# One gate of the gated MLP moved to the next stage, its mixing in another set of banks, one bias operation for two heads

## The chip, the core and the metric

The kernel runs on one core of a Trainium2 chip. The metric is the time of one execution on the device in microseconds; the median of three runs before the change is 690.52 us.

## What is computed

A layer norm of x (1024 x 1024), then one mixer layer: a combined projection of 3912 columns feeds four head groups, each multiplied by its own gate, concatenated, projected out and normalised. Cut to what matters here:

```
proj = x @ w_in + b_in            # a_u a_v a_g | bq bk bv bg | cq ck cv cg | iq ik iw | mq mg
ya = gelu(a_u) * (W_s LN(gelu(a_v)) + b_s)         # A: 128 x 128 mixing per channel group
yb = softmax(q k' / 8 + relative bias) v           # B: own chunk and 8 chunks before, 4 heads
score = sum_h relu(iq_h . ik / 8) * iw_h / sqrt(8) # index scores of 8 heads
idx = top 256 keys of each query by score          # C: attention to those alone, 4 heads
yc = softmax(q k_idx' / 8 + bias[idx]) v_idx
ym = softmax(q km' / 8) vm                         # M: 256 memory tokens, 4 heads
mixed = concat(ya * silu(a_g), yb * silu(bg), yc * silu(cg), ym * silu(mg))
out = LN(alpha * x + mixed @ w_out + b_out)
```

All is float32; a projection is made of three matmuls per 128 rows of weights (high part times high part, high times low, low times high).

## The kernel before, in words

The work lies in stages that follow each other in program order, and the framework draws the order of each engine's queue at compile time: it takes instructions by their place in the program (earlier is more urgent; some blocks are raised or lowered) as soon as they are ready in its own simulated time. The engines then run these fixed queues in order. So an instruction of a later stage can stand as filling between those of an earlier one.

**Index stage** (line 516). The words of `INDEX_ORDER` (line 56) are done in turn: `q2` projects a pair of index queries (`iq_tile`, line 455: one load of weights, projections of 256 and 512 columns), `h1` forms the scores of a pair of index heads for all keys (`index_heads`, line 462: matmuls into two banks per piece, relu on ACT, weighted sum on DVE), `a0` is the first half of group A's gate (`gate_of_a`, line 485): two weight blocks, for each half of the positions a gelu of a_u and a silu of a_g, their product on POOL and its store to DRAM. `a1` is the second half and stands in `EARLY`, with the second pair of memory gates `m0`, `m1`.

**The stage that follows** (line 1105): `early_steps` runs `EARLY` and the projection of the memory queries. It is woven (`weave`, line 657) with the search for the 256th largest score: `search` (line 977) settles one bit of a threshold per step. A step ("test" below) writes `cand`, counts scores above it (three blocks of rows on ACT as `jka`, three on DVE as `jk`) and settles `bit` and `thr`. Search steps have the lowest priority of all (`PRI`), and a step may not stand ahead of what was last on DVE and ACT four parts (`LAG_S`) before it. `PACE` says how many steps go with each of five weaves: the early steps, the memory attention of two pairs of heads, the band attention (B) of two pairs. `count` (line 1110) is the number of parts of the first weave, 8 for each projection.

**The two weaves of memory attention** take as filling the projections for A's v rows and for B (`first_filler`, `second_filler`, lines 919 and 938). Between them stand four groups of A's mixing (`a_mix`, line 823): 16 matmuls into one bank `pm`, an add of the table on DVE (`amix`), a product with the stored gate on POOL, a store.

**Banks.** PSUM's eight banks are shared by name (`BANKS`, line 68): `pp` 2 (projections, and here the mixing), `qk` 2 and `pt` 3 (scores of the first and second head of a pair; `pt` also serves every second product with V, all turning of tiles, and gating), `pv` 1.

**Band and sparse attention** (`mix_of`, line 703). `scores` writes the scores of two heads, adds bias and keeps running maxima in `mx` (one DVE operation per piece and head), then for each head forms the Exp's bias `nb` = 14 ln 2 - max on DVE and calls Exp on ACT. In group B, POOL splits the result in two 16-bit parts, and a DMA turns it.

Of the kernel before, what the change touches and what calls it, by code (L numbers as in the profile page):

```python
# [18 lines left out]
AF = mybir.ActivationFunctionType  # L19
ALU = mybir.AluOpType  # L20
# [4 lines left out]
P = 128  # L25
# [8 lines left out]
PSHIFT = 14.0 * math.log(2.0)  # L34
# [18 lines left out]
HR_S4 = 3  # L53
WO_V = 2
LAG, LAG_T, LAG_S, LAG_C = 22, 15, 4, 6
INDEX_ORDER, EARLY = "h0 q2 h1 a0 q3 h2 h3", "a1 m0 m1"
B0_ORDER, B1_ORDER, C0_PROJ = "g0 v1 g1 k0 k1", "q0 q1 k0 k1 v0 g0 v1 g1", "k0 k1 q0 q1 v0 g0 v1 g1"
RATES = (48, 64, 64, 64)
PRI = 10 ** 6
PACE = ((6,), (8,), (8,), (11,), (16,))  # L60
MASKS = (6, 7, 5), (4, 3, 2)
C1_STEPS = 40
C1_ORDER, C1_HELD, HELD_PARTS, HELD_STEPS = "k0 k1 v1 q1 v0 g1", "q0 g0", 5, 16
# [15 lines left out]
def tile_trunk(ctx, tc, x, mem, ln_in_g, ln_in_b, w_in, b_in, a_ln_g, a_ln_b, a_ws, a_bs,  # L79
# [23 lines left out]
    PE, V, S = Engine(nc.tensor), Engine(nc.vector), Engine(nc.scalar)  # L103
# [33 lines left out]
    bias = cp.tile([P, 31], F32, name="bias")  # L137
# [33 lines left out]
    def small(shape, name, bufs=3):  # L171
        return gp.tile(list(shape), F32, tag=name, bufs=bufs, name=name)
# [13 lines left out]
    def bank(tag, name=None):  # L186
        return ps.tile([P, 512], F32, tag=tag, bufs=BANKS[tag], name=name or tag)
# [82 lines left out]
    def two_banks():  # L270
        return bank("qk"), bank("pt", "qk")

    def pieces_of(n):
        return {640: ((0, 384), (384, 640)), 768: ((0, 384), (384, 768)), 896: ((0, 384), (384, 896)),
                1024: ((0, 512), (512, 1024))}.get(n, ((0, n),))
# [252 lines left out]
    def spread(pt, n):  # L528

        t = gp.tile([P, 10, P], F16, tag="pT", bufs=TB, name="pT")  # L530
        ph, pl = [t[:, a:a + 4].rearrange("p j q -> p (j q)") for a in (0, 4)]
        S.activation(ph[:, :n], pt[:, :n], AF.Copy)
        V.tensor_sub(pl[:, :n], pt[:, :n], ph[:, :n])
        return [ph[:, j * P:(j + 1) * P] for j in range(n // P)], [pl[:, j * P:(j + 1) * P] for j in range(n // P)]
# [168 lines left out]
    def mix_of(kt, rb, kb0, st, near, far_of, last):  # L703

        by_dma = kt < 4
        q, k, v3 = st
        nk = rb + 1 - kb0
        n = nk * P
        nfar = max(0, n - 256)
        chunks = list(range(0, nk, 4))  # L710
        d = {}

        def scores():
            d["rsum"] = small([P, 2], "rsum", 5)
            d["sc"] = [gp.tile([P, 1024], F32, tag="S", bufs=SB, name="sc") for _ in range(2)]
            mx = [small([P, 4], "mx", 4) for _ in range(2)]
            nr = [near(odd) for odd in range(2)]
            nmx = [0, 0]
            pieces = [(a, b) for a, b in pieces_of(n)]
            for group in [pieces] if by_dma else [[piece] for piece in pieces]:  # L720
                banks = [two_banks() if by_dma else (bank("qk"), bank("qk")) for _ in group]
                two_heads(q, k, [(accs, 0, b - a, rb * P, kb0 * P + a) for accs, (a, b) in zip(banks, group)])
                for (a, b), accs, odd in [(*x, odd) for x in zip(group, banks) for odd in range(2)]:
                    for lo, hi in ((a, min(b, nfar)), (max(a, nfar), b)):
                        if lo >= hi:
                            continue
                        other = far_of(lo, hi) if hi <= nfar else nr[odd][:, 256 - n + lo:256 - n + hi]
                        i = nmx[odd]
                        V.tensor_tensor_reduce(d["sc"][odd][:, lo:hi], accs[odd][:, lo - a:hi - a], other, 0.125,
                                               mx[odd][:, i - 1:i] if i else -3e38, ALU.add, ALU.max, mx[odd][:, i:i + 1])  # L730
                        nmx[odd] += 1
            for odd in range(2):
                sc, i = d["sc"][odd], nmx[odd]
                nb = small([P, 1], "nb")
                V.tensor_scalar(nb, mx[odd][:, i - 1:i], -1.0, PSHIFT, ALU.mult, ALU.add)
                S.activation(sc[:, :n], sc[:, :n], AF.Exp, bias=nb, accum_out=d["rsum"][:, odd:odd + 1])
                if by_dma:
                    d["p", odd] = turned(sc, n)

        def turn(odd, c):  # L740
            sc = d["sc"][odd]
            m = min(4, nk - c)
            pt = bank("pt")
            for j in range(m):
                PE.transpose(pt[:, j * P:(j + 1) * P], sc[:, (c + j) * P:(c + j + 1) * P], ident)
            d["p", odd, c] = spread(pt, m * P)

        def values(odd, c):
            if not odd and not c:
                d["pv"] = bank(("pv", "pt")[rb % 2 and by_dma], "pv")  # L750
            ph, pl = [part[c:] for part in d["p", odd]] if by_dma else d["p", odd, c]
            for j in range(min(4, nk - c)):
                pv_mm(d["pv"], odd, ph[j], pl[j], v3[:, kb0 + c + j, odd], c + j == 0, c + j == nk - 1)
            if odd and c == chunks[-1]:
                d["o"] = normalized(d["pv"], d["rsum"], kt)

        def close():
            last(lambda dst: gated(d["o"], gate_of(kt, rb), dst))

        steps = [(odd, c) for odd in range(2) for c in chunks]  # L760
        return [Item(scores, [] if by_dma else [lambda s=s: turn(*s) for s in steps], [lambda s=s: values(*s) for s in steps], close)]


# [59 lines left out]
    def a_mix(vts, i, r2):  # L823
        if i not in gates_a:
            gates_a[i] = [gp.tile([P, 512], F32, tag="near", bufs=2, name="gate_a") for _ in range(2)]
            for p in range(2):
                SP.dma_start(out=gates_a[i][p], in_=gate_dram[p][i])
        pm = bank("pp", "pm")
        for r in range(2):
            for g in range(4):  # L830
                PE.matmul(pm[64 * (g % 2):64 * (g % 2) + 64, (2 * r + g // 2) * P:(2 * r + g // 2 + 1) * P],
                          vts[:, r, g * 64:g * 64 + 64], wsT[:, g, :], start=True, stop=True)
        t = ev("amix").rearrange("p (r t c) -> p r t c", r=2, t=2)
        V.tensor_add(t, pm.rearrange("p (r t c) -> p r t c", r=2, t=2), bsT.unsqueeze(1).to_broadcast([P, 2, 2, P]))
        for r in range(2):
            rb = 4 * i + 2 * r2 + r
            for p in range(2):
                G.tensor_mul(t[:, r, p], t[:, r, p], gates_a[i][p][:, (rb % 4) * P:(rb % 4 + 1) * P])
            SP.dma_start(out=mix_dram[rb][:, 0:2, :], in_=t[:, r])
# [131 lines left out]
    for i, rb in enumerate(RBS):  # L971
        n = (rb + 1) * P
# [84 lines left out]
    for i, rb in enumerate(RBS):  # L1057
        n = (rb + 1) * P
# [43 lines left out]
    def pace(i):  # L1102
        return [(f, n) for f, n in zip(topk, PACE[i])]

# [274 lines left out]
```

## Time and profile before

| | before |
|---|---|
| median of 3 runs | 690.52 us (689.62 to 691.79) |
| profiled execution | 689.95 us, its span 688.2 us |
| mean granted TensorE clock | 0.982 |
| PE busy | 644.5 us, 94% |
| DVE busy | 516.0 us, 75% |
| ACT busy | 392.8 us, 57% |
| POOL busy | 351.6 us, 51% |

Busy times are of one execution under the hardware profiler. A PE row's end is modelled, and rows of matmuls that follow each other overlap. Engines: PE matmuls, PEld weight loads, DVE vector, ACT scalar, POOL GpSimd, SP the queue that issues DMAs. All operations on PE, DVE and ACT go through one recorder and carry its line, L94, so groups are told apart by the names of their tiles: `acc` a projection, `qk` scores, `pm` the mixing, `amix` its add.

### The profile page before, as it was taken

The numbers are of one execution on the slowest core, as the hardware profiler recorded it, in microseconds if no ns is written. First come the engines' busy times: TensorE is split into PE (matmuls) and PEld (weight loads), VectorE is DVE, ScalarE is ACT, GpSimd is POOL, SyncE is SP. The second block draws the span as 40 slices with busy tenths as digits, with TensorE's granted clock in tenths as the row PEclk, the third lists the DMA queues.
The fourth block names the chain that finished last, engine by engine and source line by source line (L and its number), as shares of the span: only waits on it lengthen the run. The fifth ranks groups of instructions, "written<-read, shape, count | busy, mean of one in ns | idle before, by whom it ended". The sixth has DMA issues, their size and how long they took to land.

```text
span 688.2 us, 11110 instructions
## 1 busy us (share of the span) xinstructions
PE 644.5 (94%) x3698; PEld 487.8 (71%) x3698; DVE 516.0 (75%) x1286; ACT 392.8 (57%) x801; POOL 351.6 (51%) x362
## 2 busy tenths in 40 slices
PE   4989999999999985979989999999999999999995
PEld 3857876776777764767767766677777777777785
DVE  6585245655777897899799789996567789889735
ACT  4665336554777867875978886444345474444210
POOL 3672311631538775474556355984222455559752
PEclk9999999999999997999999999999999999999998
DMA  9792610411236442445356535654001564143111
GB/s 275 232 335 68 168 31 1 122 32 47 72 96 123 97 126 62 86 118 142 79 108 144 94 92 107 131 98 117 30 21 54 162 198 171 65 136 148 63 61 62
DMA packets 121669, 75.30 MB, mean 109 GB/s; under 512 B 58976, under 2 KB 111500, under 8 KB 121612
## 3 DMA queue, kind: packets, MB, share of 16 engines
q1 hardware_dynamic: 121612, 74.59, 39.9%
q8 instruction: 29, 0.48, 0.3%
q14 instruction: 28, 0.23, 0.1%
HBM read 46.44 MB, written 17.64 MB: 93 GB/s over the span
## 4 chain that ended last, share of the span: by engine, by line
PE 53%; DVE 20%; ACT 8%; issue 5%; DMA 2%; POOL 2%; DVEq 0%; POOLq 0%; SPq 0%; ACTq 0%
PE acc L94 40%; PE qk L94 7%; ACT jka L94 4%; DVE jk L94 4%; PE pv L94 4%; PE pt L94 2%; DVE sc L94 2%; DVE o L94 2%; DVE nb L94 2%; DVE cand L94 1%; DMA raw<-in_w_in 1%; ACT sc L94 1%; DVE thr L94 1%; DVE bit L94 1%; DVE vt L94 1%
## 5 line engine op out<-in xcount | busy, mean ns | idle before, releaser
L94 PE MATMUL acc<-hTh,wblk 128*128 128x512 f32 (+1 forms) x960 | 324.3, 405 | 12.9 <-DVE amix L94 11.5
L94 PEld LDWEIGHTS acc<-hTh,wblk 128*128 128x128 f32 x960 | 180.3, 192 | 61.8 <-DVE amix L94 12.3
L94 PE MATMUL acc<-hTl,wblk 128*128 128x512 f32 (+1 forms) x480 | 191.3, 399 | 0.0
L206 POOL TENSOR_TENSOR wblk<-raw,wblk 128x512 fp32r<-128x512 f32 x72 | 99.5, 1386 | 95.9 <-ACT wblk L94 93.9
L94 ACT ACTIVATE jka<-score,cand 128x768 int8<-128x768 f32 (+2 forms) x93 | 96.7, 1040 | 21.9 <-DVE cand L94 19.5
L94 PEld LDWEIGHTS acc<-hTl,wblk 128*128 128x128 f32 x480 | 92.3, 192 | 18.7 <-issue 1.4
L94 ACT ACTIVATE sc<-sc,nb 128x640 f32<-128x640 f32 (+7 forms) x64 | 46.6, 731 | 48.0 <-DVE nb L94 34.4
L94 PEld LDWEIGHTS <-pT 128*128 128x128 f16 x656 | 45.4, 98 | 29.5 <-issue 21.5
L94 DVE SCALAR_TENSOR_TENSOR score<-relu,iw,score 128x384 f32<-128x384 f32 (+5 forms) x42 | 44.8, 1071 | 20.7 <-ACT relu L94 18.1
L94 ACT ACTIVATE wblk<-raw 128x512 fp32r<-128x512 f32 x72 | 44.6, 627 | 24.3 <-PE acc L94 17.2
L544 POOL TENSOR_TENSOR sc<-sc 128x512 f16<-128x512 f32 (+4 forms) x48 | 57.1, 1196 | 1.8
L94 PE MATMUL pv<-v,pT 128*128 128x192 bf16 (+1 forms) x528 | 54.6, 234 | 1.5 <-DMA pT<-sc 1.5
L94 PE MATMUL acc<-woh,mh 128*128 128x512 f32 (+1 forms) x144 | 55.6, 386 | 0.0
L94 PE MATMUL acc<-woh,ml 128*128 128x512 f32 (+1 forms) x144 | 53.5, 373 | 0.2 <-DVE nb L94 0.2
L94 PE MATMUL acc<-wol,mh 128*128 128x512 f32 (+1 forms) x144 | 53.6, 372 | 0.0
L94 ACT ACTIVATE relu<-qk 128x384 f32<-128x384 f32 (+2 forms) x80 | 36.2, 527 | 26.5 <-PE qk L94 26.3
L543 POOL TENSOR_SCALAR sc<-sc 128x512 f16<-128x512 f32 (+4 forms) x48 | 33.8, 708 | 33.2 <-ACT sc L94 32.8
L94 ACT ACTIVATE pT<-pt 128x512 f16<-128x512 f32 (+3 forms) x48 | 22.3, 483 | 36.6 <-PE pt L94 33.4
L94 DVE TENSOR_SCALAR_CACHE_REDUCE jk<-planes,lo 128x384 bf16<-128x384 uint16 (+2 forms) x48 | 35.7, 744 | 1.1
L94 PE MATMUL qk<-kh,qh 64*128 64x384 f32 (+3 forms) x96 | 31.9, 411 | 2.6 <-DVE mx L94 1.6
L94 DVE TENSOR_SCALAR_CACHE_REDUCE jk<-planes,cand 128x384 bf16<-128x384 bf16 (+2 forms) x45 | 33.3, 739 | 0.6
L1146 POOL TENSOR_TENSOR comb<-score,nearC 128x256 f32<-128x256 f32 x24 | 18.5, 784 | 27.1 <-DVE mx L94 24.8
(205 smaller groups left out, 1250.3 us busy)
## 6 DMA issues: line engine op xcount, KB each, us to landing
raw<-in_w_in SPq DMA_DIRECT2D x32, 512.0 KB, 3.7
xt<-in_x SPq DMA_DIRECT2D x8, 512.0 KB, 4.6
h_dram<-xt SPq DMA_DIRECT2D x8, 512.0 KB, 5.6
gate<-t SPq DMA_DIRECT2D x16, 256.0 KB, 2.0
rawo<-in_w_out SPq DMA_DIRECT2D x8, 512.0 KB, 4.8
hr<-h_dram SPq DMA_DIRECT2D x8, 512.0 KB, 4.6
out<-hr SPq DMA_DIRECT2D x7, 512.0 KB, 2.6
gate<-gate SPq DMA_DIRECT2D x48, 64.0 KB, 2.0
```

The source lines that it names most:

```text
L94: ins = op(*a, **k)
L206: G.tensor_sub(t[:, 1], r, f32(t[:, 0]))
L543: G.tensor_scalar(high, sc[:, :n], 1.0, 0.0, ALU.mult, ALU.add)
L544: G.tensor_sub(rest, sc[:, :n], high)
L1146: G.tensor_add(t, score[rb][:, n - 256:n], nearC[pair][:, odd, :])
```

## The change

Three edits. The word `a0` goes from the index stage's order to the front of `EARLY`, so that the search's first weave has 96 parts instead of 64; `PACE` is drawn anew, with the same total of 49 steps. The mixing's bank `pm` is taken from `pt` instead of `pp`. In `mix_of`, the maxima of both heads lie in one tile, and one DVE operation forms the biases of both before either Exp; the tile `mx` has three buffers for two heads (before: four for one), `nb` three for two heads (before: three for one).

```diff
-INDEX_ORDER, EARLY = "h0 q2 h1 a0 q3 h2 h3", "a1 m0 m1"
+INDEX_ORDER, EARLY = "h0 q2 h1 q3 h2 h3", "a0 a1 m0 m1"
...
-PACE = ((6,), (8,), (8,), (11,), (16,))
+PACE = ((10,), (7,), (7,), (10,), (15,))
...
-            mx = [small([P, 4], "mx", 4) for _ in range(2)]
+            mx = small([P, 2, 4], "mx")
...
                         V.tensor_tensor_reduce(d["sc"][odd][:, lo:hi], accs[odd][:, lo - a:hi - a], other, 0.125,
-                                               mx[odd][:, i - 1:i] if i else -3e38, ALU.add, ALU.max, mx[odd][:, i:i + 1])
+                                               mx[:, odd, i - 1:i] if i else -3e38, ALU.add, ALU.max, mx[:, odd, i:i + 1])
                         nmx[odd] += 1
+            nb = small([P, 2], "nb")
+            V.tensor_scalar(nb, mx[:, :, nmx[0] - 1], -1.0, PSHIFT, ALU.mult, ALU.add)
             for odd in range(2):
-                sc, i = d["sc"][odd], nmx[odd]
-                nb = small([P, 1], "nb")
-                V.tensor_scalar(nb, mx[odd][:, i - 1:i], -1.0, PSHIFT, ALU.mult, ALU.add)
-                S.activation(sc[:, :n], sc[:, :n], AF.Exp, bias=nb, accum_out=d["rsum"][:, odd:odd + 1])
+                sc = d["sc"][odd]
+                S.activation(sc[:, :n], sc[:, :n], AF.Exp, bias=nb[:, odd:odd + 1], accum_out=d["rsum"][:, odd:odd + 1])
...
-        pm = bank("pp", "pm")
+        pm = bank("pt", "pm")
```

## Rows read from the trace of the kernel before

**Rows 1.** The page, part 1: busy us, share of span, instructions.

```profile
PE 644.5 (94%) x3698; PEld 487.8 (71%) x3698; DVE 516.0 (75%) x1286; ACT 392.8 (57%) x801; POOL 351.6 (51%) x362
```

**Rows 2.** Busy time by stage: stretch, length, each engine, clock, DMA share, GB/s.

```profile
84.00:187.00 103.00, 102.89 (x560) 74.98 (x556) 60.58 (x74) 56.80 (x118) 31.70 (x24) 1.00 0.19 54
187.00:308.00 121.00, 106.54 (x633) 82.47 (x629) 101.50 (x265) 94.34 (x208) 78.46 (x101) 0.96 0.44 102
308.00:331.00 23.00, 23.00 (x105) 17.86 (x106) 20.89 (x58) 14.92 (x28) 11.69 (x16) 0.93 0.48 124
331.00:450.00 119.00, 114.40 (x664) 81.87 (x663) 107.97 (x370) 86.21 (x175) 71.54 (x76) 0.99 0.51 106
450.00:650.00 200.00, 196.88 (x1175) 147.03 (x1174) 161.22 (x400) 92.38 (x199) 104.38 (x90) 0.99 0.35 109
```

**Rows 3.** Chain of waits, shares by line, of 84:187, 187:308 and 308:331.

```profile
by line: PE acc L94 73.0%; PE qk L94 24.1%; ACT t L94 1.2%; issue 0.6%; ACT wblk L94 0.6%; PE wst L94 0.6%; ACT xh L94 0.0%
...
by line: ACT jka L94 15.4%; DVE jk L94 11.1%; issue 8.5%; DVE nb L94 7.6%; DVE vt L94 5.6%; PE acc L94 5.2%; DVE cand L94 4.6%; DVE thr L94 4.3%; ACT sc L94 4.0%; ACT score L94 3.8%; DVE bit L94 3.6%; DVE score L94 3.2%; DMA raw<-in_w_in 2.
...
by line: PE acc L94 89.5%; PE pv L94 5.0%; PE qk L94 2.5%; PE vt L94 1.9%; PE pt L94 1.5%
```

**Rows 4.** PE in order of time: start us, us, what, count.

```profile
93.74 0.39 PE L94 MATMUL acc<-hTl,wblk 128*128 128x512 f32 x1
...
94.44 0.40 PE L94 MATMUL acc<-hTl,wblk 128*128 128x512 f32 x1
...
201.50 0.51 PE L94 MATMUL qk<-km,mqh 64*128 64x256 f32 x4
```

**Rows 5.** Chain of waits, pieces of the index stage: start us, us, what.

```profile
132.29 7.29 PE acc L94 x37
...
156.37 3.70 PE acc L94 x15
```

**Rows 6.** DVE in order of time: starts of tests of the search.

```profile
195.44 0.17 DVE L94 TENSOR_SCALAR cand<-thr 128x6 uint32<-128x6 uint32 x1
...
205.68 0.17 DVE L94 TENSOR_SCALAR cand<-thr 128x6 uint32<-128x6 uint32 x1
...
324.44 0.16 DVE L94 TENSOR_SCALAR cand<-thr 128x6 uint32<-128x6 uint32 x1
...
329.03 0.17 DVE L94 TENSOR_SCALAR cand<-thr 128x6 uint32<-128x6 uint32 x1
```

**Rows 7.** Groups of instructions, DVE: count, busy us, mean ns, idle before.

```profile
L94 DVE TENSOR_SCALAR_CACHE_REDUCE jk<-planes,cand 128x384 bf16<-128x384 bf16 (+2 forms) x45 | 33.3, 739 | 0.6
...
L94 DVE SCALAR_TENSOR_TENSOR t<-t,xh 128x512 f32<-128x512 f32 x24 | 20.4, 852 | 8.9 <-ACT t L94 8.9
...
L94 DVE TENSOR_SCALAR cand<-thr 128x6 uint32<-128x6 uint32 x31 | 11.0, 356 | 0.6
...
L94 DVE TENSOR_TENSOR bit<-c,bar 128x6 uint32<-128x6 f32 x31 | 10.9, 351 | 17.2 <-ACT jka L94 16.9
...
L94 DVE SCALAR_TENSOR_TENSOR thr<-bit,thr 128x6 uint32<-128x6 uint32 x31 | 9.2, 296 | 0.6
...
L94 DVE TENSOR_SCALAR nb<-mx 128x1 f32<-128x1 f32 x64 | 8.1, 144 | 0.0
```

**Rows 8.** Waits: who, for whom, us in all, times, longest.

```profile
PE acc L94 <- DVE amix L94: 11.5, 3, 6.9
```

**Rows 9.** In order of time: the mixing's add, projections that waited for it.

```profile
267.61 0.69 DVE L94 TENSOR_TENSOR amix<-pm,atab 128x512 f32<-128x512 f32 x1
...
268.35 0.80 PE L94 MATMUL acc<-hTh,wblk 128*128 128x512 f32 x1 [6.90 <-DVE amix L94]
...
307.98 0.80 PE L94 MATMUL acc<-hTh,wblk 128*128 128x512 f32 x1 [3.68 <-DVE amix L94]
```

**Rows 10.** DVE in order of time: a bias, then a score operation.

```profile
333.19 0.15 DVE L94 TENSOR_SCALAR nb<-mx 128x1 f32<-128x1 f32 x1
333.26 0.42 DVE L94 CUSTOM_DVE_ANT_0 sc<-qk,nearB 128x256 f32<-128x256 f32 x1
```

## The prediction

> **What bounds the kernel now.** I read the page's two first parts, then a table of busy time by stage, then the chain of waits in each stage, then single stretches. The page has PE at 94% and DVE at 75% [rows 1], which alone would say: PE sets the time, and work that only moves from one stretch of PE to another is worth nothing. The table and the chain say something else. In 84:187, the index stage, PE is busy 102.89 of 103 us and DVE 60.58 [rows 2], and the chain is PE: 73.0% projections, 24.1% index scores [rows 3]. In 187:308, the search with the memory attention, DVE is busy 101.50 of 121 and ACT 94.34, and the chain is spread over the search's tests on ACT (15.4%) and DVE (11.1%) and a tail of small DVE steps; PE's projections have 5.2% of it. In 308:331 the chain is PE again (89.5%). In 331:450 DVE is busy 107.97 of 119. In 450:650 PE is busy 196.88 of 200. So the bound alternates: PE, DVE with ACT, PE, DVE, PE.
>
> PE's busy share also overstates it: two hTl matmuls with two others between them start 0.70 us apart, so one takes 0.233 us of the array, while its own row says 0.39 [rows 4]. The Trainium skill (Perfetto Trace Analysis, Identifying the Most-Contended Engine) says the same, that matmul busy time is no measure of headroom and weight-load time is the better one; the page's 71% for weight loads [rows 1] agrees. By the 94% the move would give nothing (the third rival below), by the 71% PE has room in 187:308.
>
> **The sum's base.** The profiled execution took 689.95 us (span 688.2, 1.75 around it), 0.57 under the median of 690.52. Terms are taken from 689.95; at the end 0.57 is added. A measurement of this kernel tells about 0.3% (2.1 us) from no change.
>
> **Part 1: the gate a0 leaves the index stage.** It is 4 projections of 24 matmuls, 96 x 0.233 = 22.4 us of PE, and two weight blocks, four evictions, two POOL products and two stores with it. It does not vanish: the same matmuls now have lower priority than q3, h2 and h3, as a1, m0 and m1 have today. Those already run inside the index stage as filling: between two bursts of index scores PE does 15 projection matmuls in 3.70 us [rows 5]. Filling is still at hand (a0 takes the place that a1 has), so I expect the heads h1 to h3 to keep their rhythm. What goes is the one place where PE does nothing but projections on the way to the last index score: 37 matmuls, 7.29 us from 132.29, the end of a0 and all of q3, which h2 follows [rows 5]. q3 then becomes filling of h0 and h1. So the last index score comes 7.3 us sooner (bounds: 0, if a0 only changes places with q3; 22.4, if none of a0 is done before the last score).
>
> The first memory scores, at 201.50 [rows 4], do not come sooner: all projections in front of them are the same, and PE stands at none of them. So in these 7.3 us the search works on DVE and ACT beside PE's projections. A test of the search beside projections took 4.6 us (324.44 to 329.03 [rows 6]); 7.3 / 4.6 = 1.6 tests are done early. Today one test starts (195.44) before 201.50 and the second at 205.68, although six are allowed in that weave, so it is the late scores and not PACE that hold the search; I cost the new PACE at nothing for that reason. It costs as much as the lead is worth if the tests do come as fast as it allows. In 187:308 DVE is in the chain, so each test that is gone from it gives back its DVE time: 3 counts x 0.739 + 0.356 + 0.351 + 0.296 = 3.2 us [rows 7]. 1.6 x 3.2 = **-5.1 us** (bounds: 0 to -15.6, that is 22.4 / 4.6 = 4.9 tests).
>
> Moved with it: the evictions are four t products of 0.852 us on DVE [rows 7], now perhaps beside the search. Before 201.50 DVE is idle for 42 of 103 us [rows 2], so I cost them at nothing; without that cover, +3.4. The two weight loads are moved past that of q3 in SP's queue and their splits past q3's on ACT and POOL; both engines are about half idle or more in 84:187 (56.80 and 31.70 of 103), so nothing is added. The two stores of a0 go later in SP's queue; their reader, the product behind the mixing's adds, stands far behind (the second add is at 267.61 [rows 9]).
>
> **Part 2: the mixing's bank.** The four a_mix groups today take one of the two pp banks of the projections and hold it until DVE adds the table. DVE has the search queued in front of that add. PE waits for it three times, 11.5 us in all, the longest 6.9 [rows 8]: at 268.35 it had waited 6.90 for the add of 267.61, at 307.98 another 3.68 [rows 9]. With a bank from the three of pt, the next projection finds a pp bank free. For the first two waits I count nothing: they lie inside the stretch whose chain is DVE and ACT. The third opens the stretch 308:331, which is PE alone; there 3.7 us are **-3.7 us**. The granted clock is 0.93 in that stretch [rows 2], 1.6 us of 23 that may come back as well; I leave it out, since the clock is also under 1 in 331:450 where no mixing is. Bounds: 0 (the wait moves to another bank) to -11.5 - 1.6 = -13.1.
>
> By the Trainium skill (Perfetto Trace Analysis, Matmuls) independent groups should rotate through different banks, so that one's eviction overlaps the next one's matmuls. By it the whole 11.5 would go, and that sum is a rival below.
>
> **Part 3: one bias operation.** 64 nb operations become 32. They take 8.1 us in all, 0.127 each [rows 7]; 16 of those removed lie in 331:450, where DVE is the bound: -2.0. The other 16 lie behind 450, beside PE: nothing. Against it, the first head's Exp now waits until the second head's scores are written. Often both nb stand back to back; where they don't, as behind 333.19, a score operation of 0.42 us lies between [rows 10], and ACT, then POOL's split and the turning DMA of the first head come 0.4 later. If that were so 16 times and always in the chain, +6.7. Taking it for a few places, I put the part at **-1.0 us** (bounds -2.0 and +4.7).
>
> **Sum.** 689.95 - 5.1 - 3.7 - 1.0 = 680.15, and with 0.57 for the median 680.7 us.
>
> **The rivals** (times with the 0.57).
> - *The index stage empties.* PE's order may put none of a0 in front of the last index score. For it: a0 has the lowest priority of what stands there. Against: a1 with the same priority fills today, and a matmul costs nothing where PE would wait for ACT to free a bank. Lead 22.4 us, 4.9 tests, -15.6 - 3.7 - 1.0: 670.2 us.
> - *All mixing waits are worth their length.* If PE, running ahead in 250:308, brings the projections of the band stage forward so that the PE-bound stretch 308:331 begins that much earlier and is that much shorter, all 11.5 us count: 689.95 - 5.1 - 11.5 - 1.0 + 0.57 = 672.9. For it: that stretch is made of exactly these projections. Against: they can run ahead only as far as two pp banks and their evictions on DVE allow, and DVE is the one that is late. It is the result that the rotation rule above would give.
> - *Nothing moves.* PE's work is the same, the lead is eaten since the attention's own steps on ACT, POOL and DMA, not the search, set 187:308, and PE picks up its waits elsewhere; what is left is part 3: 690 (688.5 to 691). For it: 94% PE on the page; tests stand in the chain with small pieces only, the largest share being 15.4%. Against: rows 2 and 3.
> - *Slower: the mixing stops the attention.* pt also serves the second head's scores, every second PV product, every gating transpose and the turning of V and of the gate rows. A pt bank that waits for DVE behind the search can hold up one of these instead of a projection, and behind that PE instruction, in order, stand the scores that DVE, ACT and POOL wait for. Price: the 11.5 us that PE waits today, now in the chain: 689.95 + 11.5 - 5.1 - 1.0 + 0.57 = 695.9. It decides from the point at which PE asks for a third pt bank between a mixing and its add. For it: the add was up to 6.9 us late and each memory item asks for pt four times. Against: three banks, and at 268.35 what PE wanted next was a projection.
>
> **How the numbers follow.** Forecast 680.7 (own range 674 to 687): 0.43. Emptied index stage: 0.10. All mixing waits: 0.10. Nothing moves: 0.17, of which 0.02 go to faster. Slower: 0.20. Faster by over 0.3%: 0.43 + 0.10 + 0.10 + 0.02 = 0.65; within 0.3%: 0.15; slower: 0.20. For 8 in 10 the range must reach most of the faster rivals (670.2) and of the slower one (695.9) with some room for the order of all queues being drawn anew: 668 to 697.
>
> **What would show it.** Part 1: in the profile after, no run of 37 projection matmuls between h1 and h2, the last index score near 180 instead of 187, the first memory scores still near 201, and the third test started by then. If the last index score is near 165, the first rival. Part 2: the row of waits of PE's projections for amix gone, and no wait of some us for a pt bank (by the add, by a gating product or by nb) in its place; the stretch between the end of memory attention and the first band scores begins and ends earlier. Part 3: 32 nb operations of about the same 0.13 us. The prediction is wrong if the first memory scores come later than 202, if PE waits for DVE in 250:310 as long as before, or if the gain that is there at 331 is given back by 450, since the tests that are then still to come lie in the band stage.

## The result, and the profile after

The changed kernel takes 686.24 us (median of 6 runs, 684.75 to 688.17) against 690.60 (6 runs); the ratio is 0.9935, 95% interval 0.9915 to 0.9954. Timed again later beside other runs of before it was 0.9968 (0.9950 to 0.9986). So it is faster, by 0.3 to 0.65%, 2 to 4.5 us; forecast were 9.8. The two timings of this one kernel differ by 0.33%, so in what follows a difference of that size between kernels timed apart is at the edge of what can be told. The profiled execution has a span of 685.0 us, before 688.2. The table by stage, as [rows 2] (the page's first row first):

```profile
PE 641.4 (94%) x3698; PEld 485.2 (71%) x3698; DVE 523.8 (76%) x1254; ACT 390.8 (57%) x801; POOL 349.9 (51%) x362
...
84.00:187.00 103.00, 100.01 (x554) 74.02 (x553) 69.17 (x96) 60.71 (x123) 28.16 (x22) 1.00 0.17 47
187.00:308.00 121.00, 114.34 (x671) 88.50 (x669) 101.78 (x257) 95.64 (x215) 82.94 (x103) 0.99 0.46 106
308.00:331.00 23.00, 22.05 (x117) 16.12 (x116) 22.00 (x71) 15.25 (x31) 11.11 (x16) 1.00 0.59 147
331.00:450.00 119.00, 111.82 (x645) 79.96 (x641) 104.73 (x324) 79.69 (x163) 70.97 (x76) 0.97 0.49 104
450.00:650.00 200.00, 195.96 (x1176) 145.52 (x1176) 162.99 (x387) 92.97 (x199) 104.45 (x92) 1.00 0.35 108
```

Three things changed against [rows 2]. PE now has a gap in the index stage (100.01 of 103 where it was 102.89). In 187:308 PE is busier (114.34 for 106.54), and DVE is as busy as before (101.78 for 101.50), although tests were to leave this stretch. In 308:331 the granted clock is 1.00 for 0.93, and the chain is no longer PE's: the shares by line of that stretch begin

```profile
by line: DVE jk L94 28.2%; issue 19.6%; DMA gate<-gate 8.5%; DVE thr L94 7.2%; DVE sc L94 4.8%; DVE o L94 4.5%; DVE mix L94 4.1%; POOL amix L838 3.7%; DVE planes L94 3.5%; DVE lo L94 3.4%; DVE vr L94 3.0%; DVE bit L94 2.7%; DVE cand L94 2.7
```

that is, the search (`jk`, `thr`, `lo`, `bit`, `cand`), where [rows 3] had 89.5% projections.

PE in order of time in the changed kernel (start, us, what, in brackets idle time and what ended it): a wait in the index stage, the last index score, the first memory scores, the first band scores:

```profile
121.34 0.50 PE L94 MATMUL acc<-hTh,wblk 128*128 128x512 f32 x1 [2.06 <-DVE iql L94]
...
171.14 0.40 PE L94 MATMUL qk<-ikl,iqh 64*128 64x512 f32 x2
...
204.12 0.50 PE L94 MATMUL qk<-km,mqh 64*128 64x256 f32 x4
...
322.23 0.33 PE L94 MATMUL qk<-kh,qh 64*128 64x128 f32 x1
```

In the kernel before, the last index score and the first band scores:

```profile
186.99 0.39 PE L94 MATMUL qk<-ikl,iqh 64*128 64x512 f32 x2
...
328.38 0.33 PE L94 MATMUL qk<-kh,qh 64*128 64x128 f32 x1
```

The last index score is 15.9 us sooner than before (forecast 7.3, bounds 0 and 22.4), but the first memory scores are 2.6 us later than in [rows 4]. How far the search runs ahead shows in the starts of its tests

```profile
182.35 0.17 DVE L94 TENSOR_SCALAR cand<-thr 128x6 uint32<-128x6 uint32 x1
...
203.56 0.17 DVE L94 TENSOR_SCALAR cand<-thr 128x6 uint32<-128x6 uint32 x1
...
208.89 0.17 DVE L94 TENSOR_SCALAR cand<-thr 128x6 uint32<-128x6 uint32 x1
```

These are the first, fourth and fifth; in [rows 6] one started before the memory scores. PE's waits between memory scores and 331 (who, for whom, us in all, times, longest) hold no mixing any more, against 11.5 us in [rows 8]:

```profile
PE pv L94 <- DMA pT<-sc: 3.2, 2, 2.4
PE qk L94 <- DVE mix L94: 2.0, 1, 2.0
PE pv L94 <- DVE o L94: 1.6, 1, 1.6
PE avt L94 <- DVE mix L94: 0.5, 1, 0.5
```

The clock goes with it. Where PE stood for the mixing, the granted clock fell, in these two stretches of before and of after:

```profile
260.00:270.00 10.00, 3.10 (x19) 2.17 (x14) 8.97 (x26) 8.44 (x24) 3.52 (x6) 0.67 0.05 15
270.00:280.00 10.00, 10.00 (x36) 7.59 (x36) 5.20 (x12) 6.05 (x14) 9.46 (x11) 0.82 0.91 190
```

```profile
260.00:270.00 10.00, 10.00 (x70) 7.99 (x69) 8.60 (x26) 7.88 (x24) 6.26 (x11) 1.00 0.29 78
270.00:280.00 10.00, 10.00 (x64) 7.82 (x63) 6.56 (x12) 7.01 (x15) 7.05 (x8) 1.00 0.92 184
```

Before, PE was busy 3.10 of 10 us and then ran below full clock for some us more (0.82 in the next 10): this wait of PE cost its length and some slow matmuls behind it.

The stages can be read from three Exps on ACT: the first of the first band pair, of the second, of group C. Before, then after:

```profile
333.38 0.40 ACT L94 ACTIVATE sc<-sc,nb 128x128 f32<-128x128 f32 x1 [0.32 <-DVE nb L94]
...
404.88 0.40 ACT L94 ACTIVATE sc<-sc,nb 128x128 f32<-128x128 f32 x1
...
472.72 0.40 ACT L94 ACTIVATE sc<-sc,nb 128x128 f32<-128x128 f32 x1
```

```profile
330.23 0.41 ACT L94 ACTIVATE sc<-sc,nb 128x128 f32<-128x128 f32 x1 [0.30 <-DVE nb L94]
...
407.87 0.39 ACT L94 ACTIVATE sc<-sc,nb 128x128 f32<-128x128 f32 x1
...
471.08 0.40 ACT L94 ACTIVATE sc<-sc,nb 128x128 f32<-128x128 f32 x1
```

So it is 3.2 us ahead of before at 330, 3.0 us behind at 408, 1.6 ahead at 471, and 3.2 at the end of this execution.

### The profile page after: what moved, and what is told of

Its sections match the earlier page's. It is cut to its first block, busy times and chain, and to the rows that moved or that the text cites. A ratio compares the mean times of both kernels' runs of the same rounds, so it can differ in the third digit from the quotient of the medians.

```text
span 685.0 us, 11070 instructions
## 1 busy us (share of the span) xinstructions
PE 641.4 (94%) x3698; PEld 485.2 (71%) x3698; DVE 523.8 (76%) x1254; ACT 390.8 (57%) x801; POOL 349.9 (51%) x362
## 4 chain that ended last, share of the span: by engine, by line
PE 48%; DVE 20%; ACT 11%; issue 5%; DMA 4%; POOL 3%; DVEq 0%; POOLq 0%; ACTq 0%; SPq 0%
PE acc L94 34%; PE qk L94 7%; ACT jka L94 5%; DVE jk L94 4%; PE pv L94 4%; PE pt L94 2%; ACT sc L94 2%; DVE nb L94 2%; DMA pT<-sc 2%; DVE thr L94 2%; DVE sc L94 1%; DVE o L94 1%; DVE bit L94 1%; DVE cand L94 1%; DVE score L94 1%
## 5 line engine op out<-in xcount | busy, mean ns | idle before, releaser
L94 PE MATMUL acc<-hTh,wblk 128*128 128x512 f32 (+1 forms) x960 | 320.9, 402 | 4.2 <-DVE iql L94 2.6
L94 PEld LDWEIGHTS acc<-hTh,wblk 128*128 128x128 f32 x960 | 178.3, 190 | 50.5 <-issue 8.0
L94 PEld LDWEIGHTS acc<-hTl,wblk 128*128 128x128 f32 x480 | 90.9, 189 | 18.8 <-issue 2.8
L94 DVE SCALAR_TENSOR_TENSOR score<-relu,iw,score 128x384 f32<-128x384 f32 (+5 forms) x42 | 43.8, 1059 | 22.4 <-ACT relu L94 20.6
L544 POOL TENSOR_TENSOR sc<-sc 128x512 f16<-128x512 f32 (+4 forms) x48 | 55.5, 1164 | 1.7
L94 PEld LDWEIGHTS acc<-woh,mh 128*128 128x128 f32 x144 | 27.2, 189 | 5.8 <-issue 1.1
```

What stands on the lines that cost most here:

```text
L94: ins = op(*a, **k)
L544: G.tensor_sub(rest, sc[:, :n], high)
```

## The experiments

The table has all kernels: ratio to before with its 95% interval; then lengths of stages in us, from one execution each: I from 84 to the first memory scores (`qk<-km`), M from there to the first band scores (`qk<-kh`), F to the first band Exp, B0 to the second pair's first Exp, B1 to group C's first Exp, R to the end of the span; last the tests of the search that were still to start at the first band Exp. "Gate" is `a0` moved with the new `PACE`. The second execution of the changed kernel tells how well a stage repeats: M, F and B1 within 0.1, B0 within 1.6, I within 1 (the clock falls there in some executions).

```
kernel                      ratio  95% interval      I     M     F    B0    B1     R  tests
before                      1                     117.5 126.9   5.0  71.5  67.8 215.5  13
after                       0.9935 .9915-.9954    120.1 118.1   8.0  77.6  63.2 213.9  12
after_2 (after again)       0.9968 .9950-.9986    121.0 118.0   8.0  76.0  63.3 214.4  12
gate (old PACE)             1.0053 1.0032-1.0074  119.4 126.5   5.4  72.8  70.6 216.4  12
gate_pace                   1.0025 1.0000-1.0051  120.7 126.5   5.4  71.4  68.1 217.3  12
bank                        1.0072 1.0047-1.0098  118.4 116.4   9.3  79.2  71.4 215.2  15
bias                        1.0037 1.0016-1.0058  118.0 126.7   5.2  72.0  70.9 215.2  13
no_bias (gate+bank)         1.0009 .9988-1.0029   119.9 117.8   7.8  74.7  68.7 215.4  12
no_bank (gate+bias)         1.0007 .9990-1.0024   120.5 126.4   5.4  73.2  65.4 214.6  12
bank_bias                   1.0079 1.0057-1.0102  117.7 116.3   9.7  77.6  72.2 215.3  15
redraw (of before)          1.0026 1.0001-1.0050  117.4 125.8   6.3  74.0  71.8 215.5  13
bank_r (redraw of bank)     0.9943 .9915-.9972    117.6 114.0   8.0  74.1  71.0 215.4  15
after_r (redraw of after)   0.9999 .9976-1.0023   119.1 124.9   6.1  71.1  68.9 213.6  11
after_g (redraw of after)   0.9970 .9947-.9992    121.5 117.6   6.7  75.0  66.8 213.4  12
before_m4                   1.0031 1.0018-1.0043  117.6 125.5   4.6  75.0  68.3 214.5  11
bank_m4                     1.0010 .9990-1.0030   118.0 122.4   4.2  77.7  67.9 215.3  11
gate_pace_m4                0.9943 .9918-.9968    120.5 124.7   4.7  69.9  65.4 215.2   7
after_m4                    0.9926 .9897-.9956    122.6 122.3   4.3  72.5  64.0 214.7   7
after_pv                    0.9900 .9872-.9928    119.3 119.1   7.5  76.0  63.2 215.6  12
after_pv_2 (again)          0.9910 .9894-.9926    117.0 117.8   7.6  76.3  63.2 214.8  12
```

**Each part alone.** Part 1 without and with the new allowance, part 2, part 3, each put into the kernel before:

```diff
-INDEX_ORDER, EARLY = "h0 q2 h1 a0 q3 h2 h3", "a1 m0 m1"
+INDEX_ORDER, EARLY = "h0 q2 h1 q3 h2 h3", "a0 a1 m0 m1"
```

> The gate a0 moved alone, with the search's allowance per weave as it was (6, 8, 8, 11, 16) and the two other parts undone. Theory A (the prediction's): the lead of the search comes from the empty index stage alone, and each early test is worth 3.2 us of DVE: last index score near 171 as in the changed kernel, 4 tests started by the first memory scores, 5 us under the kernel before. Theory B (the allowance places the tests): with the old allowance the tests do not come earlier than today, and the time is within 2 us of before. Theory C (the search's start is worth less than its DVE time): tests start early as in A, and the gain is 1 to 3 us.

> The gate a0 moved with the new allowance (10, 7, 7, 10, 15), the mixing still in a projection bank and two bias operations: part 1 of the prediction whole. Theory A: -5.1 us against before, the mixing's waits still there. Theory B: -4 us, that is all the gain of the whole change, since the other parts are worth nothing. Theory C: 0 to -2 us, since the mixing's waits hold up the projections that now stand in this stage; then part 2 is what makes part 1 pay.

```diff
-        pm = bank("pp", "pm")
+        pm = bank("pt", "pm")
```

> The mixing's bank alone. Theory A (the prediction's): the wait of 3.7 us at 308 goes and 3.7 us are gained, the two others are covered. Theory B: PE was not what ended that stage, the wait moves, and the time is within 1 us of before. Theory C: a pt bank held by the mixing stops the memory attention: 2 to 6 us slower.

```diff
-                nb = small([P, 1], "nb")
-                V.tensor_scalar(nb, mx[odd][:, i - 1:i], -1.0, PSHIFT, ALU.mult, ALU.add)
+            nb = small([P, 2], "nb")
+            V.tensor_scalar(nb, mx[:, :, nmx[0] - 1], -1.0, PSHIFT, ALU.mult, ALU.add)
```

> One bias operation for two heads alone. Theory A (the prediction's): 16 operations less where DVE is the bound, -1.0 us, between -2.0 and +4.7. Theory B: the first head's exponential, its split and its turning transfer come later by one score operation, and the band stage is the longer by it: +1 to +3 us; then it is this part that gives the change's gain back between 331 and 407. Theory C: nothing, within 0.7 us.

None of the four is faster than before; three are slower by 0.4 to 0.7%, and every theory on gate and on gate_pace expected less time or about the same. The premises of theory A hold in gate: last index score at 170.5, four tests started by the memory scores, and that with the old allowance, so `PACE` indeed does not hold the search there. Its conclusion falls: M is 126.5 where it was 126.9, and I is 2 to 3 us longer, which stands undiminished in the first band Exp (335.3 and 336.5 for 333.4). Three tests more lie ahead of the memory scores, but later ones moved up: in M and F together 15 tests start instead of 17. Even those two gave back nothing. From the first memory scores to the first band Exp, before and then gate, both take 131.9 us (as do gate_pace and no_bank with their 15 tests and bias with its 17), and DVE is busy 1.6 us longer in gate:

```profile
201.50:333.38 131.88, 112.98 (x306) 0.95 0.46 107
203.42:335.28 131.86, 114.54 (x296) 0.96 0.46 107
```

(Stretch, length, DVE's busy time and instructions, clock, DMA.) The durations of the search's operations add up to 3.8 us less there, those of the others, as many but one, to 3.2 us more (the eight `vt<-nat,mv,atab` alone 2.1), so DVE's time did not come free. In bank the first band scores come 9.7 us earlier and the first Exp 5.3, more than the 3.7 forecast, and then B0 and B1 take 11.3 us longer. The 5 us lost are those of theory C, but not by its way: the memory attention is 10.5 us shorter, and the loss lies behind it. There PE waits (of 328:408, as above):

```profile
PE pt L94 <- DVE mx L94: 4.0, 1, 4.0
PE pv L94 <- DMA pT<-sc: 1.9, 2, 1.3
PE qk L94 <- DVE mx L94: 1.9, 2, 1.2
PE pt L94 <- DVE o L94: 1.2, 1, 1.2
```

for score operations on DVE (`mx`), in whose queue the 15 tests still to come stand. In bias, where 2.0 us were to be saved in 331:450, B0 is 0.5 and B1 3.1 us longer; the time is in the range of theory B. The bias operations themselves did not get cheaper. In bias, and in the changed kernel, they are

```profile
L94 DVE TENSOR_SCALAR nb<-mx 128x2 f32<-128x2 f32 x32 | 12.0, 376 | 0.2
L94 DVE TENSOR_SCALAR nb<-mx 128x2 f32<-128x2 f32 x32 | 10.9, 341 | 0.4
```

so half as many operations take more of DVE than the 8.1 us of [rows 7].

**All pairs, and a redraw.** The changed kernel with one part undone, before with parts 2 and 3, and before with nothing but the order of two row blocks inside the mixing turned round:

```diff
-        for r in range(2):
+        for r in (1, 0):
             for g in range(4):
                 PE.matmul(pm[64 * (g % 2):64 * (g % 2) + 64, (2 * r + g // 2) * P:(2 * r + g // 2 + 1) * P],
```

> The changed kernel with two bias operations again (gate moved, new allowance, mixing in its own bank). Theory S (two bounds in one stretch: the early tests bring nothing while the mixing's waits hold PE, and PE's freed waits bring nothing while the search is late, so that either alone is lost and both together count): 4 to 8 us under the kernel before, and 2 to 3 us under the changed kernel, since the bias alone cost 2.6. Theory N (the order of all queues is drawn anew with every edit, and the draw moves the time by some us whatever the edit): anywhere within 6 us of before, with no relation to the parts' own times. Theory I (the bias part is what makes the two others pay, since it frees DVE in the band stage): 1 us or more over the kernel before.

> The changed kernel with the mixing in a projection bank again (gate moved, new allowance, one bias operation). Theory S: slower than before by 2 to 5 us (1.7 of the gate and its allowance alone, 2.6 of the bias alone), first band exponentials at 334 to 337. Theory N: within 6 us of before on either side. Theory I: 2 us or more faster than before.

> The kernel before with the mixing's bank and the one bias operation, the gate where it was. Theory S: slower than before by 5 to 9 us (5.0 and 2.6 alone), band stage begun 4 to 5 us early, that lead gone by 405, and the search's last test at 425 or later. Theory N: within 6 us of before on either side. Theory I: at or under the time of before.

> The kernel before with the two row blocks of each mixing group computed in the other order: the same instructions, the same tiles, the same waits, only the order that the planner then draws for the queues behind the first mixing differs. It measures what a new order alone is worth. Theory S: within 1.5 us of before, so that the parts' own times of 2 to 5 us are theirs. Theory N: 2 to 6 us off, on either side, so that no difference of that size between two of these kernels belongs to a part.

No pair is faster than before: gate and bank, gate and bias are equal to it, bank and bias 0.8% slower. Single parts of +0.25, +0.7 and +0.4% that make -0.3 to -0.65% together add up in no way. Theory S foresaw bank_bias alone; it missed no_bank by 2 us and no_bias by 5. Theory I missed no_bank and bank_bias. Theory N, that any of them lies within 6 us of before, holds for all three, but it excludes little. Up to the first band Exp the parts of these eight kernels do add up, within 2 us: the gate makes I 1.5 to 3 us longer, the bank makes M 8 to 11 shorter and F 2.4 to 4.5 longer, the bias changes none of them. The disorder is in B0 and B1. The redraw has the same instructions and is 0.26% slower, 1.8 us, between the two theories' ranges (its profiled execution, span 694.7, was the slowest of its twelve runs, as was that of gate, so their stages overstate the time).

**What a test costs.** Four kernels with four of the search's tests left out. In the traces `cand` is written from `thr` 31 times, so 27 of 31 are left, not 28 of 32 as the expectations have it; these kernels leave out a part of the search and give another result:

```diff
-        for b in range(30, 15, -1):
+        for b in range(26, 15, -1):
```

> The kernel before with the search's first four tests left out (bits 30 to 27 of the threshold are not tested; 28 tests instead of 32, and the masks are those of another threshold). It prices a test. Theory P (the prediction's price: 3.2 us of DVE each wherever the chain runs through DVE): 12.8 us under before. Theory S (the search stands in the way behind the first band scores only; up to them PE's order sets the time): first band exponential still at 333 to 334, and 5 to 9 us gained behind it. Theory Z (the tests lie beside other work): under 2 us.

> The mixing's bank alone, with the search's first four tests left out. Alone with the whole search it cost 5 us (1.0072), although its band stage began 5 us earlier, with 15 tests still to come instead of 13. Theory S (its lead is eaten by the search that is then late): with four tests fewer the sign turns, 2 to 6 us under the kernel before with four tests fewer, first band exponential at 323 to 328. Theory K (the bank itself costs in the band stage, by what waits for pt, or by the order drawn): still 3 to 6 us over the kernel before with four tests fewer. Theory P: 5 us over it, exactly its own loss.

> The gate moved with the new allowance, with the search's first four tests left out, mixing and bias as before. Theory S: nothing at the first band exponential (336 as with the whole search, since PE's order sets it and the late first memory scores cost 2.6 us), and the same gain behind it as the kernel before has from four tests fewer, so 1 to 3 us over the kernel before with four tests fewer. Theory P: 12.8 us under its own time with the whole search. Theory K: no prediction of its own.

> The changed kernel with the search's first four tests left out. Theory S: here DVE with the search ends the memory stage too, so the first band exponential comes sooner (324 to 328 instead of 330), and more is gained than by the kernel before: 8 to 13 us under the changed kernel. Theory P: 12.8 us under it. Theory Z or K: the search ended early enough already (403 instead of 413), so under 4 us.

At 3.2 us a test each would gain 12.8 us, 1.9%. The measured changes of ratio are +0.3% for before, -0.6 for bank, -0.8 for gate_pace and -0.1 to -0.4 for the changed kernel: 2 us on average for four tests, with a scatter of 4. Theory P is out, in all four. Theory S gave ranges too and missed them: before_m4 gains nothing behind the first band Exp, bank_m4 is 1.5 us under before_m4 where 2 to 6 were expected, gate_pace_m4 6 us under it where it was to be 1 to 3 over, and the changed kernel gains 0.6 to 2.9 us instead of 8 to 13, its first band Exp at 333.1 where 324 to 328 were expected. The four tests do not leave the memory attention, which is why it says little on their price there: in all twenty executions 14 to 16 tests start in M (16 in before, 15 in before_m4, 16 in gate_pace_m4), the later ones moving up. What sets that number was not tested. Behind M there is a trend: B0 and B1 together take 135 to 137 us with 7 tests to come, 139 to 146 with 11 to 13, and 145 to 151 with 15. That is some 12 us for 8 tests, 1.5 each, read over kernels that differ in more than their tests; not every kernel obeys it: before_m4 has two tests fewer to come than before, and its B0 is longer.

**Redraws of after and of bank.** The same turn of row blocks as in redraw, put into the changed kernel and into bank, and another turn of order (the groups, `for g in (3, 2, 1, 0)`) in the changed kernel:

> The changed kernel with the two row blocks of each mixing group computed in the other order: the same instructions, another order of the queues behind the first mixing. Theory D (the draw is worth some us): the gain of 4.4 us does not stand, the time is 1.5 us or more over the changed kernel's 685.2. Theory S (the parts need each other, and the gain belongs to the three together): within 1.5 us of the changed kernel, 684 to 687.

> The changed kernel with the four groups of each mixing computed in the other order (a second redraw). Theory D: 1.5 us or more off the changed kernel's 685.2, and apart from the first redraw too; the spread of the three is the draw's. Theory S: within 1.5 us of it.

> The mixing's bank alone (1.0072 of before, 5 us slower) with the two row blocks of each mixing group in the other order. Theory D: the loss is in part the draw's, and goes down or up by 1.5 us or more. Theory S: the loss stays 4 to 6 us, with 15 tests to come at the first band exponential and PE idle for 7 to 8 us in each of the two band weaves.

This is the strongest result. With not one instruction more or less, bank goes from 0.7% slower than before to 0.6% faster: 9 us. So one of the three edits alone, in another draw, is as fast as the whole change. The changed kernel goes from 0.9935 and 0.9968 to 0.9970 and to 0.9999. Theory D holds for bank_r and after_r; for after_g it holds against the first timing and not against the second. How much a turn draws anew can be counted: of DVE's some 1270 instructions, when the two queues are laid side by side, about 100 stand elsewhere in redraw, 350 in bank_r, 450 in after_r, 280 in after_g. Two places show what a draw does. In after_r the fourth mixing got its pt bank such that a product of the memory attention stands behind it on PE:

```profile
311.72 1.23 PE L94 MATMUL pv<-v3m,pT 128*128 128x192 bf16 x8 [5.48 <-DVE amix L94]
```

This is the mechanism of the prediction's slower rival, and M is 124.9 there instead of 118. (bank_m4 has the same wait, 3.2 us, and M 122.4; after_g has it with 1.4 us and M 117.6; but after_m4 has M 122.3 without it.) And bank differs from its redraw in 331:450, first bank, then bank_r:

```profile
331.00:450.00 119.00, 106.22 (x596) 75.07 (x597) 109.44 (x351) 83.59 (x168) 61.73 (x67) 0.94 0.49 102
```

```profile
331.00:450.00 119.00, 111.93 (x647) 79.10 (x647) 113.08 (x356) 85.44 (x170) 67.65 (x71) 1.00 0.51 108
```

Both have 15 tests to come. bank_r gets 51 more matmuls done in the same 119 us, and its clock does not fall; its longest wait of PE in B0 is 1.9 us, that of bank 4.0.

**A version that beats both.** In the changed kernel q3's projections follow q2's on the two pp banks, and both banks are held until DVE has written `iql`: at 102.18 q3's first piece waits 0.6 us for q2's, at 121.34 the next projection waits 2.1 us for q3's. The bank pv, which a0's silu used there, is free now. The changed kernel, with the second piece of q2 and of q3 in pv:

```diff
-            run(parts_half(t, I_Q + j * P, q, a, b))
+            run(parts_half(t, I_Q + j * P, q, a, b, "pv" if j > 1 and a == 512 else "pp"))
```

> The changed kernel with the second pieces of the projections q2 and q3 in the bank that a0 leaves free in the index stage, instead of a projection bank: it takes away what makes PE wait there for the eviction (2.6 us in the changed kernel, none before). If that wait is what makes the first memory scores late, they come at 201 to 202 instead of 204.1. Theory A (the index stage's end sets what follows): 2 to 3 us under the changed kernel. Theory B (DVE with the search ends the memory stage once the mixing has its own bank): the first band exponential stays at 329 to 331, and the time within 1 us. Theory D: 1.5 us or more off on either side, with no such stage showing it.

> The changed kernel once more, for a comparison on one chip with the version with a free bank. Expected within 0.2% of its first ratio, 0.9935; first memory scores at 204, first band exponential at 330, as in its first profile; the lengths of the two band weaves (77.6 and 63.2) are expected to differ from the first profile by up to 3 us each if one execution differs from the next there.

> The changed kernel with the free bank in the index stage once more. If its gain is real, 1.5 to 3 us under the changed kernel on the same chip; if the first comparison was between chips only, within 1 us of it.

The wait is gone; PE's waits of 84:205 are now

```profile
PE acc L94 <- DVE iql L94: 0.3, 1, 0.3
PE acc L94 <- ACT atab L94: 0.3, 1, 0.3
PE acc L94 <- ACT t L94: 0.3, 1, 0.3
```

and 0.9910 (0.9894 to 0.9926) stands against 0.9968 on the same chip, medians of 682.50 and 686.67: 4.2 us under the changed kernel, at 682.5 the fastest of all. (after_2 itself missed its expectation, within 0.2% of 0.9935.) The first memory scores come at 201.0 in the second execution, the first band Exp at 326.4, and from there on the stages have the lengths of after: M, F, B0 and B1 are 0.2, 0.4, 0.3 and 0.1 us off after_2's. In the first execution they came at 203.3, with the clock at 0.70 in 50:60, which lies ahead of the edit. In five of the ten profiled executions with the wait the granted clock behind it is low as well (0.83 in 120:130, after_2 among them), in none of the ten without. Those five have I of 120.5 to 122.6, the other five 119.1 to 120.5: there the wait seems to have cost more than its length. This edit leaves the queues nearly as they were (2 of DVE's 1254 instructions stand elsewhere, 10 of ACT's 801, none of POOL's, some 160 of PE's 3698), so a draw is a poor rival here, and its gain is carried to the end: theory A, though 4.2 us are more than the 2 to 3 that it gave. Theory B, that the search would hold the first band Exp at 330, holds for the first execution (329.9) and not for the second.

## Why the prediction was right or wrong

The sign was right and the time lies in the range; the size was wrong, 4.4 us or less for 9.8. The sign is no merit of the sum: none of the three parts, put alone into the kernel before, makes it faster, and a neutral turn of the changed kernel is as slow as before.

- **Part 1, the step that failed.** "In 187:308 DVE is in the chain, so each test that is gone from it gives back its DVE time." The lead came, twice as long as forecast and between the forecast and the first rival, and so did the early tests: four instead of the 2.6 counted. But M stayed at 124.7 to 126.9 in all kernels with the mixing in pp. In gate two tests fewer start before the first band Exp, where 1.6 were counted, and instead of 6.4 us they gave nothing: the stretch takes 131.9 us as before and DVE is busy 114.5 us in it, not less than the 113.0 of before. The third early test only let a later one move up. Shares of the chain as in [rows 3] (11 and 15%) say that tests stand in it in pieces; they do not say that the stage gets shorter without them. What a test costs in the band stage, some 1.5 us, is read from a scatter.
- **Part 1, the 37 matmuls.** What is called "the end of a0 and all of q3" is a wrong reading of [rows 5]: they are the last 13 of q3's 24 narrow matmuls (256 columns) and its 24 wide ones; a0 was done by 130. So nothing of a0 stood in the stretch whose length was taken for the lead.
- **Part 1, "PE stands at none of them".** The first memory scores came 2.6 us later, not at 201.5. The step took q3 as filling; it did not ask which banks q2 and q3 would then share. a0 had stood between them, and one half of its projections used another bank. after_pv shows it: give that bank back and the memory scores come at 201.0 instead of 204.1, in the two executions without a low clock. That they might come later than 202 stood among the prediction's own signs of being wrong.
- **Part 2, mis-sized, both ways.** Three waits, 11.5 us, were costed at 3.7. With the bank alone M is 10.5 to 12.9 us shorter (bank, bank_r), so the second rival was right about the size in M. That it is the length of the waits is not shown: in gate_pace PE waits 3.9 us for the mixing instead of 11.5, and M is 0.4 us shorter. F is 3 to 4 us longer, and B0 and B1 together are 6 to 11 longer. With the gate they are only 0 to 4 longer than before's 139.3 (after, after_2, after_g, no_bias), with 12 tests to come instead of 15. But bank_r has 15 to come and is 0.6% faster than before, so the bank's gain does not hang on the gate.
- **Part 3.** "32 nb operations of about the same 0.13 us" failed: they take 0.34 to 0.38 us each, 10.9 and 12.0 us in all where 64 took 8.1. In 331:450 DVE is busy with them for 3.70 us in bias and 3.78 before, so 0.1 us is saved there and not 2.0. Alone the part cost 2.6 us, inside its bounds: B0 and B1 are 3.6 longer in bias, 0.9 shorter in no_bank than in gate_pace, 0.9 shorter in bank_bias than in bank, 2.5 shorter in after than in no_bias. Behind 470, where it was to give nothing, R is 213.4 to 215.6 with it and 214.5 to 217.3 without. Its own worth is not settled; it is smaller than what the draws move.
- **The warning that came true.** "If the gain that is there at 331 is given back by 450": 3.2 us ahead at 330, 3.0 behind at 408. But what was named as its cause, the tests still to come, is one less than before there (12 for 13); B0's order is the other, and how much belongs to each is open.
- **What the sum lacked.** A term for the order of the queues. A neutral turn moves the time by 2 to 9 us in three of the four cases tried, which is as much as each term of the sum. By the same measure it is open how much of the 4.4 us is the change's: three draws of it have 0.995 (two timings), 0.997 and 1.000, two draws of before 1 and 1.003. How much of it would remain over many draws stays open; two or three draws of each can't say.

## What to carry to other kernels

Before a sum of terms is believed, turn something round that changes no work and see how far the time moves: where a planner draws all queues from each edit, a smaller difference can't be put down to a part by the time alone. A share of the chain is a place to look, not a price: ask of each stage which engine ends it, and test the price by leaving the work out, then count whether it has left that stage or other work has moved up. When a block of work is moved out of a stage, look at what its neighbours shared while it stood between them, banks above all.

## What the hardware showed

A short DVE operation next to POOL can take seven times as long. Before, a test's small steps, and a POOL product beside each:

```profile
392.37 1.34 POOL L206 TENSOR_TENSOR wblk<-raw,wblk 128x512 fp32r<-128x512 f32 x1
392.50 1.24 DVE L94 TENSOR_TENSOR bit<-c,bar 128x6 uint32<-128x6 f32 x1
...
398.70 0.17 DVE L94 TENSOR_TENSOR bit<-c,bar 128x6 uint32<-128x6 f32 x1 [1.31 <-ACT jka L94]
...
399.26 1.28 POOL L206 TENSOR_TENSOR wblk<-raw,wblk 128x512 fp32r<-128x512 f32 x1 [1.52 <-ACT wblk L94]
399.38 1.19 DVE L94 CAST lo<-cand 128x3 f32<-128x3 uint32 x1
```

The first `bit` begins 0.13 us after POOL's product and ends 0.03 after it; the same operation alone takes 0.17. Of the 93 such steps (`cand`, `bit`, `thr`, 31 each) of this execution, 39 begin inside a POOL operation. The 54 others take at most 0.17 us. Of the 39, the 35 beside a POOL operation of 128 columns or more all end behind it, by 0.01 to 0.11 us: what a step loses is the time that the POOL operation still has to run, so one that begins near its end loses nothing that can be seen. The other four stand beside POOL operations of one column (`rs`), take 0.15 to 0.17 us and end before them. In all twenty executions it is the same: 707 steps begin inside a POOL operation other than these narrow ones, and 3 of them end before it. What stands on DVE counts too:

```profile
L94 DVE TENSOR_SCALAR nb<-mx x64: 95/143/156, 333.2 to 632.9; 128x1 f32<-128x1 f32 x64
L94 DVE TENSOR_SCALAR nb<-mx x32: 110/169/1350, 333.7 to 634.9; 128x2 f32<-128x2 f32 x32
```

These are the bias operations of before and of bias (ns, shortest, median, longest). With one column 35 of the 64 begin inside a POOL operation and none takes over 0.16 us. With two columns 17 of 32 do, and 13 of these take over 0.2 us, up to 1.35. That is where the time went that part 3 was to save. The Trainium skill (SBUF — State Buffer, SBUF: two separate sides) has DVE and GpSimd share one port pair as a lock: against a DVE operation that uses the pair, by its mode or by two inputs from SBUF, the one that starts first holds it for its whole length and the other waits. The rows of `bit` and `lo` agree with that. The three steps of a test take 1.0 us of DVE on average instead of 0.5 alone, so some of the 3.2 us of DVE per test were POOL's time.
